# Diagonal of the keys' Gram matrix taken after the block gather; three shared buffers for split values and delta states; another bank for the first up unit

## The chip, the core and the metric

One core of a Trainium2 chip runs the whole kernel. The metric is device time in microseconds (us) of one execution; lower is better. Engines are named as in the profile: PE (TensorE; PEld its weight loads), DVE (VectorE), ACT (ScalarE), POOL (GpSimd) and SP (SyncE, which issues nearly all DMAs here).

## What is computed

A trunk of two layers (DEPTH = 2) on 512 tokens of width 1024, in float32. Each layer projects the normalised input into the parts of two branches: a gated delta rule (8 heads of 128, chunks with a triangular solve) and windowed attention (16 query heads, 2 key heads of 64, window 128). Both are projected up, gated, merged and projected out; an MLP with squared ReLU follows.

```python
def hybrid_layer(x, positions, ...):
    h = rmsnorm(x, pre_mix_g)
    proj = h @ w_in
    y_a = deltanet_branch(dn_q, dn_k, dn_v, dn_z, dn_b, dn_a, ...) @ w_up_dn
    y_b = swa_sink_branch(sw_q, sw_k, sw_v, positions, sw_sinks) @ w_up_sw
    mix = (jax.nn.sigmoid(gate_a) * y_a + jax.nn.sigmoid(gate_b) * y_b) @ w_o
    x = x + rmsnorm(mix, post_mix_g)
    h2 = rmsnorm(x, pre_mlp_g)
    ff = jnp.square(jax.nn.relu(h2 @ w_ff1)) @ w_ff2
    return x + rmsnorm(ff, post_mlp_g)

def deltanet_branch(...):
    k = l2norm(k.reshape(B, S, DN_HEADS, DN_DK))
    beta = jax.nn.sigmoid(b_in.astype(jnp.float32))

def gated_delta_rule(q, k, v, g, beta):
    kb = k * beta[..., None]
    L = jnp.where(strict, jnp.einsum('bhnid,bhnjd->bhnij', kb, k) * decay, 0.0)
    u = lax.linalg.triangular_solve(L, v * beta[..., None], ...)
```

The length of each key enters through l2norm: the keys' squares are the diagonal of the key Gram matrix K K^T, and `cj` is beta divided by (square + EPS).

## The kernel before

Weights stream from HBM through five buffers `wr`; ACT casts each to `wh` (L323), DVE makes the rest `wl = wr - wh` (L324), and PE multiplies three times per 128 rows of contraction (L339 to L341), up to four weight pieces ahead (`LOOK`). A unit of 24 matmuls of 128x512 yields a 128x512 block in a PSUM bank. Banks come from four pools: `PM` (2), `PS` (3), `PZ` (2), `PK` (1). The framework's scheduler sets the order of instructions on each engine from data dependences; within an engine they then run in that order, so a waiting instruction holds what is behind it. The SP queue likewise.

In each layer the part that the change touches runs so:

- **Block loop** (16 attention groups: 4 token tiles, 2 key heads, 2 halves). Beside each group run units from the list `MIX`: K (keys of one head, `k_unit`, L722 on), G and GA (gates). `k_unit(h)` projects and convolves the keys, reloads the decay matrix `D`, makes the Gram blocks on PE (`ps_a`, L735, the only bank of `PK`), then on DVE takes the four diagonals with a multiplication by the identity (L740), adds EPS (L742), takes `irk` by a power on POOL (L744), makes `cj` (L747, L748), scales the four blocks by `cj` and `D` into `uu` (L752) and sends `uu` to HBM (`ud`).
- An attention group makes scores on PE (`ps_s`, L892), masks them into `M` (DVE L896 or ACT L899 with DVE L900), takes maximum, exponential, sum and reciprocal (DVE L904 to L913, ACT L910), scales `M` on ACT (L916), transposes it on PE (`ps_pt`, L922), splits it (`pf`, L411, L412) and multiplies by the split values `vp` (`ps_o`, L938). `att_prep(t)` (L838) makes `vp` for the tile, in two buffers.
- **Solve** (L780 on): all 32x32 diagonal blocks are gathered as `ub` (L783) and inverted by 31 DVE steps, spread over the last attention groups, the first dense units and the eight up units of attention (`ps_us`, L1211 on).
- **Chain** (8 heads): `d_load` brings the blocks of `ud` back as `ur`, `d_inverse` completes the inverse on PE (`ps_i`) with POOL copies (L1048 to L1052), `d_chain` runs the recurrence with states `St` (four buffers of 128x128) and uses `cj` and `irk` as scales, while `d_dense` runs the value, query and gate projections of the next head.

The second layer repeats all this.

Of the kernel before, what the change touches and what calls it, by code (L numbers as in the profile page):

```python
# [20 lines left out]
P = 128  # L21
# [4 lines left out]
H = 8  # L26
# [93 lines left out]
def hybrid_trunk(ctx, tc, x, positions, pre_mix_g, dn_conv_w, dn_a_log, dn_dt_bias, dn_norm_g,  # L120
# [138 lines left out]
    vxd = dr.tile([H, P, 512], F32, name="vxd")  # L259
    gd = dr.tile([32, P], F32, name="gd")  # L260
    sd = dr.tile([H, 512], F32, name="sd")
    fd = dr.tile([H, 512], F32, name="fd")
# [257 lines left out]
    for l in range(depth):  # L520
# [130 lines left out]
        hc = lambda a: a.rearrange("p (h c) -> p h c", c=NC)  # L651
        beta = s1("beta", 32)
        act(out=hc(beta), in_=ba[:, :, 0:8].rearrange("p t h -> p h t"), func=AF.Exp, scale=-1.0)
# [18 lines left out]
        tt(out=hc(lw), in0=hc(lw), in1=nal.unsqueeze(2).broadcast_to([P, H, NC]), op=ALU.mult)  # L672
        gc, ngc, neg, egl = (s1(n_, 32) for n_ in ("gc", "ngc", "neg", "egl"))

        def decays():
            ps = PS("ps_g")
            mm(ps[:, 0:32], lhsT=le, rhs=lw, start=True, stop=True)
            nc.vector.tensor_copy(gc, ps[:, 0:32])
            ts(out=ngc, in0=gc, scalar1=-1.0, scalar2=None, op0=ALU.mult)
            act(out=neg, in_=gc, func=AF.Exp)  # L680
            ts(out=neg, in0=neg, scalar1=-1.0, scalar2=None, op0=ALU.mult)
            ps = PS("ps_gt")
            tr(ps[:32, :P], gc, ident)
            gT = sm.tile([32, P], F32, name="gT", bufs=1)
            nc.vector.tensor_copy(gT, ps[:32, :P])
            dma(gd, gT)
            egT = sm.tile([32, P], F32, name="egT", bufs=1)
            act(out=egT, in_=gT, func=AF.Exp)
            dma(egd, egT)
            for h in range(H):  # L690
                d = T[4 + h % 2]("D")
                dma(c4(d), gd[h * NC:(h + 1) * NC, :].partition_broadcast(P))
                nc.gpsimd.affine_select(out=c4(d), in_=c4(d), pattern=[[0, NC], [1, P]],
                                        compare_op=ALU.is_ge, fill=NEG, base=0, channel_multiplier=-1)
                act(out=egl[:, h * NC:(h + 1) * NC], in_=c4(d)[:, :, P - 1], func=AF.Exp)
                for c in range(NC):
                    act(out=d[:, c * P:(c + 1) * P], in_=d[:, c * P:(c + 1) * P], func=AF.Exp,
                        bias=ngc[:, h * NC + c:h * NC + c + 1])
                dma(dd[h], d)
# [21 lines left out]

        cj, irk = [], []  # L722

        def k_unit(h):
            ps = PM("ps_kp")
            mm_a(ps, hT)
            k_ = conv_silu(ps, 8 + h, T[4], "kk")
            dma(kkd[h], k_)
            yield
            d = T[5]("D")  # L730
            dma(d, dd[h])
            ps = PK("ps_a")
            for c in range(NC):
                sl = slice(c * P, (c + 1) * P)
                mm(ps[:, sl], lhsT=k_[:, sl], rhs=k_[:, sl], start=True, stop=True)  # L735
            u_ = T[5]("uu")
            sk_ = sm.tile([P, NC], F32, name="ssk")
            for c in range(NC):
                sl = slice(c * P, (c + 1) * P)
                stt(out=u_[:, sl], in0=ps[:, sl], scalar=1.0, in1=ident, op0=ALU.mult,  # L740
                    op1=ALU.mult, accum_out=sk_[:, c:c + 1])
            ts(out=sk_, in0=sk_, scalar1=EPS, scalar2=None, op0=ALU.add)  # L742
            ir = sm.tile([P, NC], F32, name="irk", bufs=H + 1)
            ptt(out=ir, in0=sk_, in1=phalf, op=ALU.pow)  # L744
            irk.append(ir)
            cc = sm.tile([P, NC], F32, name="cj", bufs=H + 1)
            nc.vector.reciprocal(cc, sk_)  # L747
            tt(out=cc, in0=cc, in1=hc(beta)[:, h, :], op=ALU.mult)  # L748
            cj.append(cc)
            for c in range(NC):  # L750
                sl = slice(c * P, (c + 1) * P)
                stt(out=u_[:, sl], in0=ps[:, sl], scalar=cc[:, c:c + 1], in1=d[:, sl],  # L752
                    op0=ALU.mult, op1=ALU.mult)
            dma(umat(h), c4(u_))
# [25 lines left out]
        def solve():  # L780
            ub = X4("ub")
            u0 = ud[:, :]
            dma(ub.rearrange("p (j i) -> p j i", j=32),  # L783
                bass.AP(u0.tensor, u0.offset, [[32 * P + 32, P], [P, 32], [1, 32]]))
            pb = X4("pb")
            nc.gpsimd.memset(pb, 0.0)
            nc.gpsimd.memset(pb[:, 0:1024:33], 1.0)
            yield
            uv = ub.rearrange("p (j i) -> p j i", j=32)
            pv = pb.rearrange("p (n i) -> p n i", n=32)  # L790
            for j in range(30, -1, -1):
                m = 31 - j

                for n0, n1 in (((0, m),) if m <= 16 else ((0, (m + 1) // 2), ((m + 1) // 2, m))):
# [7 lines left out]
                                            op=ALU.add, negate=True)  # L802
                yield
            dma(pd, pb)
            Pc, Tc = X4("Pc"), X4("Tc")
# [26 lines left out]

        def att_prep(t):
            tsl = slice(t * P, (t + 1) * P)
            kd = kv[t]

            vp = sm.tile([P, 512], F32R, name="vp")
            v4 = lambda a: a.rearrange("p (g r d) -> p r g d", g=2, r=2)  # L838
# [3 lines left out]
            for a, src in ((vp[:, 0:256], v_), (vp[:, 256:512], kd[:, 256:384]))[:1 + (t > 0)]:  # L842
                a, src = v4(a), src.rearrange("p (g d) -> p g d", g=2)
                split(src, a[:, 0], a[:, 1])
            at["v", t] = vp
            ps = PS("ps_k")
            tr(ps[:, 0:P], kd[:, 0:128], ident)
# [142 lines left out]
        def d_load(*hs):  # L990
            for h in hs:
                if h < H:
                    dma(uview(h), umat(h))

        def d_inverse(h):
# [84 lines left out]
        def d_turn(h):  # L1080
            d, k_ = dn["D", h], dn["k", h]
            kds = sm.tile([P, NC], F32, name="kds")
            tc.keep_in_program_order(tt(out=kds, in0=cj[h], in1=c4(d)[:, :, P - 1], op=ALU.mult))
            dn["k", h] = k_, by_token(k_, kvx[1][:, h % 2 * 512:(h % 2 + 1) * 512], kxd[h]), kds
# [59 lines left out]
        def d_chain(h):  # L1144
# [8 lines left out]
            for c in range(NC):  # L1153
                sl = slice(c * P, (c + 1) * P)
                stt(out=aT[:, sl], in0=ps[:, sl], scalar=cj[h][:, c:c + 1], in1=d[:, sl],
                    op0=ALU.mult, op1=ALU.mult)
# [3 lines left out]
            for c in range(NC):  # L1160
                for out_, in_, by in ((vs, vt, irk[h]), (kd, kt, kds)):
                    act(out=out_[:, c * P:(c + 1) * P].rearrange("p (a i) -> p a i", a=4),
                        in_=in_[:, :, c, :], func=AF.Copy, scale=by[:, c:c + 1])
            order.end()
            po = PZ("ps_o")
            St = None
            for c in range(NC):
# [14 lines left out]
                if c < NC - 1:  # L1182
                    pu = PS("ps_su")
                    mm(pu[:, 0:P], lhsT=kd[:, sl], rhs=yy, start=True, stop=True)
                    S2 = sm.tile([P, P], F32, name="St", bufs=4)
                    if c == 0:
# [23 lines left out]
        for m in range(KT):  # L1210
            ps = PM("ps_us")  # L1211
            mm_a(ps, oT)
# [253 lines left out]
```

## Time and profile before

| | |
|---|---|
| three runs, median (lowest to highest) | 1831.02 us (1830.64 to 1831.49) |
| the profiled execution's own time | 1830.59 us |
| its span, first to last instruction | 1828.6 us |
| granted TensorE clock | 0.999 |
| busy: PE, DVE, ACT, POOL | 99%, 71%, 51%, 12% of the span |
| block loop and solve in layer 0 | about 78 to 300 us of the span |

The span is what the trace covers; the execution's own time has 1.99 us around it. Matmuls overlap in PE's pipeline, so a PE that reads as busy can still start its matmuls later than it could. What PE loses is read from the distance between starts: in an undisturbed run of 128x512 matmuls it is 0.23 us.

### The profile page before, as it was taken

What the parts mean: (1) busy time and instruction counts of PE and PEld (TensorE: products, weight loads), DVE (VectorE), ACT (ScalarE), POOL (GpSimd) and SP (SyncE); (2) the same over time, 40 slices, a digit from 0 to 9 for tenths busy, and PEclk for the clock granted to TensorE, in tenths of its full rate; (3) what the DMA queues carried; (4) which work ended last, traced back from release to release, by engine and by line L of the source; (5) the groups of instructions that cost most, each with busy time, mean ns of one, the idle gap of its engine ahead of it and who ended that gap; (6) DMA issues with size and microseconds to landing.
All of it is one profiled execution on the core that took longest, in us unless ns stands there. A gap on an engine that the chain in (4) does not pass through costs nothing.

```text
span 1828.6 us, 26748 instructions
## 1 busy us (share of the span) xinstructions
PE 1809.1 (99%) x9598; PEld 1503.9 (82%) x9598; DVE 1292.1 (71%) x2466; ACT 940.9 (51%) x1913; POOL 211.2 (12%) x386
## 2 busy tenths in 40 slices
PE   9999999999999999999999999999999999999998
PEld 8888778888788888888898887888887898888886
DVE  5499796887566758684556997968885568585934
ACT  6678742444434645544347877234444346554442
POOL 0322102221101000000003221022111010000000
PEclk9999999999999999999999999999999999999999
DMA  5633447554453363564245343485545534544631
GB/s 188 202 118 116 115 149 223 179 170 149 124 191 124 96 216 120 168 217 151 93 151 181 104 127 110 167 234 165 160 139 153 172 119 135 174 163 148 233 102 46
DMA packets 146422, 278.48 MB, mean 152 GB/s; under 512 B 33569, under 2 KB 66657, under 8 KB 146290
## 3 DMA queue, kind: packets, MB, share of 16 engines
q1 hardware_dynamic: 145778, 276.75, 47.4%
q8 instruction: 75, 1.23, 0.3%
q14 instruction: 57, 0.47, 0.1%
q0 software_dynamic: 512, 0.03, 0.0%
HBM read 239.38 MB, written 37.36 MB: 151 GB/s over the span
## 4 chain that ended last, share of the span: by engine, by line
PE 84%; DVE 6%; ACT 5%; DMA 3%; issue 1%; POOL 1%; SPq 0%; POOLq 0%; DVEq 0%; ACTq 0%
PE ps_f L340 6%; PE ps_f L339 6%; PE ps_f L341 6%; PE ps_p L402 3%; PE ps_p L404 3%; PE ps_p L400 3%; PE ps_b L388 3%; PE ps_b L387 3%; PE ps_b L389 3%; PE ps_vp L339 2%; PE ps_us L339 2%; PE ps_ud L339 2%; PE ps_vp L341 2%; PE ps_ud L341 2%; PE ps_ud L340 2%; PE ps_us L340 2%
## 5 line engine op out<-in xcount | busy, mean ns | idle before, releaser
L323 ACT CAST wh<-wr 128x1024 fp32r<-128x1024 f32 (+1 forms) x332 | 343.1, 1040 | 542.2 <-PE ps_f L340 145.8
L324 DVE TENSOR_TENSOR wl<-wr,wh 128x1024 fp32r<-128x1024 f32 (+1 forms) x332 | 400.4, 1216 | 303.6 <-ACT wh L323 300.6
L339 PE MATMUL ps_f<-g_h,wh 128*128 128x512 f32 x448 | 174.3, 389 | 0.0
L340 PE MATMUL ps_f<-g_l,wh 128*128 128x512 f32 x448 | 174.3, 389 | 0.0
L341 PE MATMUL ps_f<-g_h,wl 128*128 128x512 f32 x448 | 174.3, 389 | 0.0
L402 PE MATMUL ps_p<-wl,P_h 128*128 128x512 f32 x336 | 131.4, 391 | 0.4 <-DVE wl L324 0.3
L404 PE MATMUL ps_p<-wh,P_l 128*128 128x512 f32 x336 | 130.8, 389 | 0.0
L400 PE MATMUL ps_p<-wh,P_h 128*128 128x512 f32 x336 | 129.5, 389 | 0.0
L437 POOL TENSOR_TENSOR pr<-pq,pw 128x1 f32<-128x1 f32 x16 | 9.8, 613 | 807.6 <-DVE pq L436 807.6
L339 PEld LDWEIGHTS ps_f<-g_h,wh 128*128 128x128 f32 x448 | 84.1, 188 | 17.4
L341 PEld LDWEIGHTS ps_f<-g_h,wl 128*128 128x128 f32 x448 | 84.1, 188 | 17.4
L340 PEld LDWEIGHTS ps_f<-g_l,wh 128*128 128x128 f32 x448 | 84.1, 188 | 17.4
L402 PEld LDWEIGHTS ps_p<-wl,P_h 128*128 128x128 f32 x336 | 63.1, 188 | 15.8 <-DVE wl L324 2.4
L400 PEld LDWEIGHTS ps_p<-wh,P_h 128*128 128x128 f32 x336 | 63.1, 188 | 13.3
L404 PEld LDWEIGHTS ps_p<-wh,P_l 128*128 128x128 f32 x336 | 63.1, 188 | 12.8
L387 PE MATMUL ps_b<-wh,h_h 128*128 128x432 f32 (+1 forms) x192 | 71.1, 370 | 0.0
L388 PE MATMUL ps_b<-wl,h_h 128*128 128x432 f32 (+1 forms) x192 | 70.5, 367 | 0.3 <-DVE wl L324 0.3
L389 PE MATMUL ps_b<-wh,h_l 128*128 128x432 f32 (+1 forms) x192 | 70.2, 366 | 0.0
L293 DVE TENSOR_TENSOR wr<-wr 128x1024 f32<-128x1024 f32 x48 | 58.0, 1220 | 2.6 <-DMA wr<-in_weights_dram 1.9
L340 PE MATMUL ps_qp<-h_l,wh 128*128 128x512 f32 x128 | 54.0, 422 | 0.0
L339 PE MATMUL ps_vp<-h_h,wh 128*128 128x512 f32 x128 | 53.9, 421 | 0.0
L341 PE MATMUL ps_vp<-h_h,wl 128*128 128x512 f32 x128 | 53.6, 419 | 0.0
(359 smaller groups left out, 4873.6 us busy)
## 6 DMA issues: line engine op xcount, KB each, us to landing
wr<-in_weights_dram SPq DMA_DIRECT2D x320, 512.0 KB, 3.5
wr<-in_weights_dram SPq DMA_DIRECT2D x24, 432.0 KB, 3.6
D<-dd SPq DMA_DIRECT2D x32, 256.0 KB, 3.2
xd<-xo SPq DMA_DIRECT2D x12, 512.0 KB, 2.8
xt<-xd SPq DMA_DIRECT2D x24, 256.0 KB, 3.7
D<-gd SPq DMA_DIRECT2D x16, 256.0 KB, 6.5
dd<-D SPq DMA_DIRECT2D x16, 256.0 KB, 3.9
kkd<-kk SPq DMA_DIRECT2D x16, 256.0 KB, 2.0
```

What stands on the lines that cost most here:

```text
L293: tt(out=held[j], in0=held[j], in1=part(i, k, j), op=ALU.add)
L323: nc.scalar.copy(wh[:, :w], wr[:, :w])
L324: sub(out=wl[:, :w], in0=wr[:, :w], in1=wh[:, :w].bitcast(F32), op=ALU.subtract)
L339: mm(ps, lhsT=wh[:, k, :], rhs=hi, start=k == 0, stop=False)
L340: mm(ps, lhsT=wh[:, k, :], rhs=lo, start=False, stop=False)
L341: mm(ps, lhsT=wl[:, k, :], rhs=hi, start=False, stop=k == KT - 1)
L387: mm(pss[t], lhsT=hi[:, tsl], rhs=wh[:, r, :], start=k == 0, stop=False)
L388: mm(pss[t], lhsT=hi[:, tsl], rhs=wl[:, r, :], start=False, stop=False)
L389: mm(pss[t], lhsT=lo[:, tsl], rhs=wh[:, r, :], start=False, stop=k == KT - 1)
L400: mm(pss[t], lhsT=hi[:, c], rhs=wh[:, r, :], start=first, stop=False, skip_group_check=onto)
L402: mm(pss[t], lhsT=hi[:, c], rhs=wl[:, r, :], start=False, stop=False, skip_group_check=onto)
L404: mm(pss[t], lhsT=lo[:, c], rhs=wh[:, r, :], start=False, stop=last, skip_group_check=onto)
```

## The change

- `k_unit` no longer takes the diagonals, `irk` and `cj`. DVE multiplies the four Gram blocks by `D` in one 128x512 operation, and the unscaled blocks go to HBM.
- `solve` adds EPS to the diagonal of the gathered blocks, makes the scale there (`sq`, 128x32) and scales `ub` by it in one 128x1024 operation. beta reaches that layout through HBM (`bd`, `bq`), the squares come back to the token layout through HBM (`nd`, then `gT`) and a PE transpose (`ps_nt`); `cj` and `irk` are then made for all heads at once, `irk` by one 128x32 power on POOL.
- `d_load` scales the four reloaded blocks of a head with four ACT operations.
- `vp` has three buffers and is made half a tile earlier (`att_values`); the delta states are slices of a tile in the same buffers.
- The first up unit's bank comes from `PS` rather than `PM`.

```diff
@@ decays
-            tr(ps[:32, :P], gc, ident)
+            tr(ps[:64, :P], gcb, ident)
...
+            dma(bd, gT[32:64])
@@ k_unit
-            sk_ = sm.tile([P, NC], F32, name="ssk")
-            for c in range(NC):
-                sl = slice(c * P, (c + 1) * P)
-                stt(out=u_[:, sl], in0=ps[:, sl], scalar=1.0, in1=ident, op0=ALU.mult,
-                    op1=ALU.mult, accum_out=sk_[:, c:c + 1])
-            ts(out=sk_, in0=sk_, scalar1=EPS, scalar2=None, op0=ALU.add)
-            ir = sm.tile([P, NC], F32, name="irk", bufs=H + 1)
-            ptt(out=ir, in0=sk_, in1=phalf, op=ALU.pow)
-            irk.append(ir)
-            cc = sm.tile([P, NC], F32, name="cj", bufs=H + 1)
-            nc.vector.reciprocal(cc, sk_)
-            tt(out=cc, in0=cc, in1=hc(beta)[:, h, :], op=ALU.mult)
-            cj.append(cc)
-            for c in range(NC):
-                sl = slice(c * P, (c + 1) * P)
-                stt(out=u_[:, sl], in0=ps[:, sl], scalar=cc[:, c:c + 1], in1=d[:, sl],
-                    op0=ALU.mult, op1=ALU.mult)
+            tt(out=u_, in0=ps, in1=d, op=ALU.mult)
             dma(umat(h), c4(u_))
@@ solve
+            bq = s1("bq", 32)
+            dma(bq, bd.rearrange("g (b j) -> (g b) j", b=4))
...
+            sq = s1("ssq", 32)
+            ts(out=sq, in0=ub[:, 0:1024:33], scalar1=EPS, scalar2=None, op0=ALU.add)
+            dma(nd.rearrange("g (b j) -> (g b) j", b=4), sq)
+            nc.vector.reciprocal(sq, sq)
+            tt(out=sq, in0=sq, in1=bq, op=ALU.mult)
+            tt(out=uv, in0=uv, in1=sq.unsqueeze(2).broadcast_to([P, 32, 32]), op=ALU.mult)
+            nT = sm.tile([64, P], F32, name="gT", bufs=1)
+            dma(nT[0:32], nd)
...
+            ps = PS("ps_nt")
+            tr(ps[:, 0:32], nT[0:32], ident[:32, :32])
+            nc.vector.tensor_copy(irk, ps[:, 0:32])
+            nc.vector.reciprocal(cj, irk)
+            tt(out=cj, in0=cj, in1=beta, op=ALU.mult)
+            ptt(out=hc(irk), in0=hc(irk), in1=phalf.unsqueeze(1).broadcast_to([P, H, NC]), op=ALU.pow)
@@ attention
-            vp = sm.tile([P, 512], F32R, name="vp")
+            vp = sm.tile([P, 512], F32R, name="vp", bufs=3)
...
             if (g, e) == (1, 0) and t < NT - 1:
+                att_values(t + 1)
                 att_rope(t + 1)
@@ d_load
                     dma(uview(h), umat(h))
+                    for c in range(NC):
+                        act(out=uview(h)[:, c, :], in_=uview(h)[:, c, :], func=AF.Copy,
+                            scale=cj[:, h * NC + c:h * NC + c + 1])
@@ d_chain
+            states = sm.tile([P, 512], F32, name="St", tag="vp", bufs=3)
...
-                    S2 = sm.tile([P, P], F32, name="St", bufs=4)
+                    S2 = states[:, sl]
@@ up units
-            ps = PM("ps_us")
+            ps = (PM if m else PS)("ps_us")
```

The scheduler lays out the instructions anew. Three places, layer 0, with line numbers of each kernel.

**PE, around the transposes of the third attention group** (`ps_pt`; the units beside it make keys, `ps_kp`). The last score block ahead of them ends at row 436 in both programs. Before:

```order
448 L341 MATMUL ps_kp<-h_h,wl 128x512
449 L339 MATMUL ps_kp<-h_h,wh 128x512
450 L922 MATMUL ps_pt<-ident,M 128x128 x4
451 L340 MATMUL ps_kp<-h_l,wh 128x512
452 L341 MATMUL ps_kp<-h_h,wl 128x512
```

Now:

```order
443 L341 MATMUL ps_kp<-h_h,wh 128x512
444 L342 MATMUL ps_kp<-h_l,wh 128x512
445 L932 MATMUL ps_pt<-ident,M 128x128 x4
446 L343 MATMUL ps_kp<-h_h,wl 128x512
447 L341 MATMUL ps_kp<-h_h,wh 128x512
```

The four transposes stand five matmuls earlier behind the score block. Most of the later groups moved the same way.

**DVE, the first `k_unit` beside the third attention group** (`M` is that group's score tile, `uu` the scaled Gram block, `kk` the next head's keys). Before:

```order
99 L742 TENSOR_SCALAR ssk<-ssk 128x4
100 L866 SCALAR_TENSOR_TENSOR qT<-ps_q,qT 64x512
101 L714 SCALAR_TENSOR_TENSOR kk<-ps_kp,cw,kk 128x511
102 L747 RECIPROCAL cj<-ssk 128x4
103 L866 SCALAR_TENSOR_TENSOR qT<-ps_q,qT 64x512
104 L718 SCALAR_TENSOR_TENSOR kk<-th,kk 128x512
105 L748 TENSOR_TENSOR cj<-cj,beta 128x4
106 L896 TENSOR_TENSOR M<-ps_s,ban 128x256
107 L752 SCALAR_TENSOR_TENSOR uu<-ps_a,cj,D 128x128 x4
108 L896 TENSOR_TENSOR M<-ps_s,ban 128x256
```

Now:

```order
97 L741 TENSOR_TENSOR uu<-ps_a,D 128x512
98 L952 TENSOR_TENSOR qt_421<-ps_o,qt_421 64x512
99 L718 SCALAR_TENSOR_TENSOR kk<-ps_kp,cw,kk 128x509
100 L874 SCALAR_TENSOR_TENSOR qT<-ps_q,qT 64x512
101 L718 SCALAR_TENSOR_TENSOR kk<-ps_kp,cw,kk 128x510
102 L874 SCALAR_TENSOR_TENSOR qT<-ps_q,qT 64x512
103 L718 SCALAR_TENSOR_TENSOR kk<-ps_kp,cw,kk 128x511
104 L906 TENSOR_TENSOR M<-ps_s,ban 128x256 x2
105 L722 SCALAR_TENSOR_TENSOR kk<-th,kk 128x512
```

`uu`, which frees the Gram bank, moved from between the two score operations to ahead of the query splits, and the two score operations stand together.

**ACT, from the up units to the chain** (`wh` are weight casts, `ur` the reloaded blocks, `vs` the first chain's values). Before:

```order
287 L1111 ACTIVATE wq<-qq 128x512
288 L323 CAST wh<-wr 128x1024 x9
289 L772 ACTIVATE sga<-ps_ga 128x512
290 L323 CAST wh<-wr 128x1024
291 L772 ACTIVATE sga<-ps_ga 128x512
292 L1162 ACTIVATE vs<-kvx,irk 128x128
```

Now:

```order
281 L1124 ACTIVATE wq<-qq 128x512
282 L325 CAST wh<-wr 128x1024 x7
283 L1005 ACTIVATE ur<-ur,cj 128x128 x15
284 L325 CAST wh<-wr 128x1024
285 L760 ACTIVATE sga<-ps_ga 128x512
286 L1005 ACTIVATE ur<-ur,cj 128x128
```

The sixteen scalings of the first four heads stand around the cast that was the ninth after the queries' square. On SP, `nd<-ssq` and `gT<-nd` now stand behind `ub<-ud` and one weight load, ahead of one `gad` store and two weight loads; `bd<-gT` stands between `gd<-gT` and `egd<-egT`.

## Rows read from the trace of the kernel before

**Rows 1.** The page: busy time of each engine, share of the span, instructions.

```profile
PE 1809.1 (99%) x9598; PEld 1503.9 (82%) x9598; DVE 1292.1 (71%) x2466; ACT 940.9 (51%) x1913; POOL 211.2 (12%) x386
```

**Rows 2.** Waits of PE, whole span: us in total, times, longest us.

```profile
PE ps_pt L922 <- ACT M L916: 3.9, 6, 0.8
...
PE ps_us L339 <- DVE qq L714: 0.6, 2, 0.3
...
PE ps_a L735 <- DVE uu L752: 0.5, 2, 0.2
...
PE ps_s L892 <- DVE M L900: 0.4, 1, 0.4
...
PE ps_b L388 <- DVE wl L324: 0.3, 1, 0.3
```

**Rows 3.** Stretches of layer 0: us, busy PE, PEld, DVE, ACT, POOL; clock; DMA.

```profile
78.00:110.00 32.00, 30.21 (x161) 24.51 (x160) 28.14 (x81) 22.21 (x70) 6.84 (x13) 1.00 0.34 103
110.00:150.00 40.00, 39.93 (x215) 32.94 (x214) 37.40 (x103) 34.81 (x101) 8.15 (x12) 1.00 0.36 118
```

**Rows 4.** Timeline of PE: start us, us, engine, line; in brackets idle before and releaser.

```profile
100.69 0.22 PE L892 MATMUL ps_s<-kT_h,qT 128*128 128x128 f32 x1
101.13 1.16 PE L735 MATMUL ps_a<-kk 128*128 128x128 f32 x8 [0.22 <-DVE uu L752]
...
107.06 0.66 PE L922 MATMUL ps_pt<-ident,M 128*128 128x128 f32 x4 [0.75 <-ACT M L916]
...
202.05 0.66 PE L922 MATMUL ps_pt<-ident,M 128*128 128x128 f32 x4 [0.51 <-ACT M L916]
...
245.57 0.39 PE L341 MATMUL ps_zp<-h_h,wl 128*128 128x512 f32 x1
246.25 0.47 PE L339 MATMUL ps_us<-oT_h,wh 128*128 128x512 f32 x1 [0.28 <-DVE qq L714]
246.55 0.40 PE L340 MATMUL ps_us<-oT_l,wh 128*128 128x512 f32 x1
246.79 0.39 PE L341 MATMUL ps_us<-oT_h,wl 128*128 128x512 f32 x1
```

**Rows 5.** Groups by line and shape, whole span: busy us, mean ns, idle before.

```profile
L740 DVE SCALAR_TENSOR_TENSOR uu<-ps_a,ident 128x128 f32<-128x128 f32 x64 | 16.1, 282 | 1.7 <-PE ps_a L735 0.8 <-issue 0.8
L752 DVE SCALAR_TENSOR_TENSOR uu<-ps_a,cj,D 128x128 f32<-128x128 f32 x64 | 17.8, 340 | 0.1
L412 DVE TENSOR_TENSOR pf_l<-ps_pt,pf_h 128x512 fp32r<-128x512 f32 x32 | 21.8, 682 | 1.8 <-ACT pf_h L411 1.5
L324 DVE TENSOR_TENSOR wl<-wr,wh 128x1024 fp32r<-128x1024 f32 x308 | 375.5, 1229 | 259.0 <-ACT wh L323 256.2 <-PE ps_pt L922 2.3
L1162 ACT ACTIVATE vs<-kvx,irk 128x128 f32<-128x128 f32 x64 | 25.0, 390 | 3.5 <-DMA kvx<-vxd 3.5
L744 POOL TENSOR_TENSOR irk<-ssk,pw 128x4 f32<-128x4 f32 x16 | 18.1, 1129 | 109.7 <-DVE ssk L742 107.3 <-DVE den L913 2.3
L437 POOL TENSOR_TENSOR nr<-nq,pw 128x1 f32<-128x1 f32 x16 | 10.6, 662 | 45.3 <-DVE nq L436 45.3
```

**Rows 6.** Timelines of SP and ACT where the blocks are gathered (start us, us).

```profile
193.13 0.36 SPq L783 DMA_DIRECT2D ub<-ud  x1
196.44 3.42 SPq L274 DMA_DIRECT2D wr<-in_weights_dram  x2
...
208.62 1.03 ACT L323 CAST wh<-wr 128x1024 fp32r<-128x1024 f32 x1
```

**Rows 7.** The chain that ended last: start us, us, a small DMA of layer 1.

```profile
1298.54 2.22 DMA ff<-sd
```

**Rows 8.** Timelines of SP, ACT, POOL and PE where the chain begins (start us, us).

```profile
287.12 2.07 SPq L993 DMA_DIRECT2D ur<-ud  x4
...
295.28 1.06 ACT L323 CAST wh<-wr 128x1024 fp32r<-128x1024 f32 x1 [4.38 <-PE ps_ga L340]
...
294.15 2.59 POOL L1050 COPY Pt<-Pc 32x128 f32<-32x128 f32 x8
...
300.84 0.21 PE L1018 MATMUL ps_i<-Tc,ur 32*32 32x32 f32 x1
```

More of the change, by code (lines that the diff above doesn't have):

```diff
@@ L260, in hybrid_trunk @@
     gd = dr.tile([32, P], F32, name="gd")
+    bd = dr.tile([32, P], F32, name="bd")
+    nd = dr.tile([32, P], F32, name="nd")
     sd = dr.tile([H, 512], F32, name="sd")
@@ L651, in hybrid_trunk @@
         hc = lambda a: a.rearrange("p (h c) -> p h c", c=NC)
-        beta = s1("beta", 32)
+        gcb = s1("gcb", 64)
+        gc, beta = gcb[:, 0:32], gcb[:, 32:64]
         act(out=hc(beta), in_=ba[:, :, 0:8].rearrange("p t h -> p h t"), func=AF.Exp, scale=-1.0)
@@ L672, in hybrid_trunk @@
         tt(out=hc(lw), in0=hc(lw), in1=nal.unsqueeze(2).broadcast_to([P, H, NC]), op=ALU.mult)
-        gc, ngc, neg, egl = (s1(n_, 32) for n_ in ("gc", "ngc", "neg", "egl"))
+        ngc, neg, egl = (s1(n_, 32) for n_ in ("ngc", "neg", "egl"))
         def decays():
@@ L682, in decays @@
             ps = PS("ps_gt")
-            tr(ps[:32, :P], gc, ident)
-            gT = sm.tile([32, P], F32, name="gT", bufs=1)
-            nc.vector.tensor_copy(gT, ps[:32, :P])
-            dma(gd, gT)
+            tr(ps[:64, :P], gcb, ident)
+            gT = sm.tile([64, P], F32, name="gT", bufs=1)
+            nc.vector.tensor_copy(gT, ps[:64, :P])
+            dma(gd, gT[0:32])
+            dma(bd, gT[32:64])
             egT = sm.tile([32, P], F32, name="egT", bufs=1)
-            act(out=egT, in_=gT, func=AF.Exp)
+            act(out=egT, in_=gT[0:32], func=AF.Exp)
             dma(egd, egT)
@@ L719, in conv_silu @@
             return a
-        cj, irk = [], []
+        irk, cj = s1("irk", 32), s1("cj", 32)
         def k_unit(h):
@@ L831, in att_rope, with att_values @@
                 ptt(out=x2, in0=tm[2], in1=tm[3], op=ALU.add)
-        def att_prep(t):
-            tsl = slice(t * P, (t + 1) * P)
+        def att_values(t):
             kd = kv[t]
-            vp = sm.tile([P, 512], F32R, name="vp")
+            vp = sm.tile([P, 512], F32R, name="vp", bufs=3)
             v4 = lambda a: a.rearrange("p (g r d) -> p r g d", g=2, r=2)
@@ L845, in att_prep @@
             at["v", t] = vp
+        def att_prep(t):
+            tsl = slice(t * P, (t + 1) * P)
+            kd = kv[t]
             ps = PS("ps_k")
@@ L874, in att_group @@
                     att_rope(0)
+                    att_values(0)
                 att_prep(t)
             if (g, e) == (1, 0) and t < NT - 1:
+                att_values(t + 1)
                 att_rope(t + 1)
@@ L1082, in d_turn @@
             kds = sm.tile([P, NC], F32, name="kds")
-            tc.keep_in_program_order(tt(out=kds, in0=cj[h], in1=c4(d)[:, :, P - 1], op=ALU.mult))
+            tc.keep_in_program_order(tt(out=kds, in0=hc(cj)[:, h, :], in1=c4(d)[:, :, P - 1], op=ALU.mult))
             dn["k", h] = k_, by_token(k_, kvx[1][:, h % 2 * 512:(h % 2 + 1) * 512], kxd[h]), kds
@@ L1154, in d_chain @@
                 sl = slice(c * P, (c + 1) * P)
-                stt(out=aT[:, sl], in0=ps[:, sl], scalar=cj[h][:, c:c + 1], in1=d[:, sl],
+                stt(out=aT[:, sl], in0=ps[:, sl], scalar=cj[:, h * NC + c:h * NC + c + 1], in1=d[:, sl],
                     op0=ALU.mult, op1=ALU.mult)
@@ L1160, in d_chain @@
             for c in range(NC):
-                for out_, in_, by in ((vs, vt, irk[h]), (kd, kt, kds)):
+                for out_, in_, by in ((vs, vt, irk[:, h * NC:(h + 1) * NC]), (kd, kt, kds)):
                     act(out=out_[:, c * P:(c + 1) * P].rearrange("p (a i) -> p a i", a=4),
```

## Prediction

> **What bounds the kernel now.** I read the page's busy times first: PE is busy for 99% of the span, DVE for 71%, ACT for 51% [rows 1]: PE is the bound. So the end moves only by what PE no longer waits for, or has to do more. Next I read what PE waits for [rows 2]: of the waits that the change can touch, the transposes `ps_pt` behind ACT's scaled scores are 3.9 us in six times, three in each layer, and the others are some tenths: the first up unit 0.6, the Gram blocks 0.5, a score block 0.4, a projection matmul 0.3. Idle time by the profile is a little too small, since it is counted from modelled ends; the distance between starts tells the rest, and there an undisturbed 128x512 matmul takes 0.23 us (246.55 to 246.79 is 0.24) [rows 4]. Last I read who is full where PE waits. In the block loop that is DVE: 28.14 of 32 us and 37.40 of 40 us, 88 and 94%, while ACT has 31 and 13% free [rows 3]. The reader is to see two things: DVE is nearly full in the block loop, so that its order decides when scores are ready; and yet PE loses very little to it, about 6 us in both layers. That is all there is to win, and it is 0.3% of the time.
>
> **The change, part by part.**
>
> *Less on DVE in `k_unit`.* Out go 64 products with the identity, 282 ns each, and 64 scaled products, 340 ns each: 16.1 + 17.8 = 33.9 us in both layers. In come 16 products of 128x512 out of PSUM; the nearest row is the split of the transposed scores, 682 ns, so 10.9 us [rows 5]. DVE is relieved of 23.0 us, 1.4 us for each of 16 units, besides three operations on 128x4 in each, and POOL of 18.1 us of powers. Most of that was never on PE's path. What was:
> - The Gram blocks wait for their single bank, which DVE's scaled products empty: the score matmul starts at 100.69 and the Gram block at 101.13 [rows 4]. `uu` now comes far ahead of that, in one operation. PE's idle time there is 0.22; with the modelled end I count 0.3 a layer, **-0.6**.
> - The third group's transposes start 0.75 us late at 107.06 [rows 4]. Between this group's two score operations and its reciprocal stood one unit's scaled products and the next unit's diagonals: 4 x 0.340 + 4 x 0.282 = 2.5 us, of which one 0.68 us operation is left, so 1.8 us less. But the scheduler has moved the transposes five matmuls, 1.15 us, nearer to the scores. 1.8 - 1.15 leaves 0.65 us; bounds are 0 (the relief lies beside the chain) and 0.75. I take 0.6, near the upper end, because the products stand on the very chain, **-1.2** for two layers.
> - The wait of a score block for DVE's masks, 0.4 us, once, in layer 1 [rows 2]: **-0.4**.
> - The transposes at 202.05, 0.51 us late [rows 4], stand beside the start of the solve; see there.
>
> *The first up unit's bank.* Its first matmul starts 0.68 us after the last of the gate projection, against 0.23, waiting for the query convolution to leave the bank (the releaser is `qq`) [rows 4]. In another pool it does not wait: 0.45 x 2 = **-0.9**. Next in line is the second up unit, which needs the same release, but 5.5 us later.
>
> *Diagonal and scale in the solve.* Added on DVE: three operations on 128x32 and one on 128x1024, for which the weight split of the same size stands, 1229 ns [rows 5]. They come where DVE has just lost the last unit's 1.8 us. Per layer the transposes at 202.05 can gain their 0.51 or lose up to 1.23 us; I take 0, as relief and addition are about equal. The solve itself ends as early or late as before within 1 us, with idle DVE behind it.
>
> *The way through HBM on the SP queue.* The store of the squares waits for the gather's landing and DVE, the load waits for the store, and one `gad` store and two weight loads stand behind both. The gather is issued at 193.13, the weight loads at 196.44 to 199.86, and the cast that begins the next weights runs at 208.62 [rows 6]. A small DMA of the chain takes 2.22 us [rows 7]. Store and load hold SP for about that each, so the second weight load comes perhaps 2 us later and lands still before 208.62. The Trainium skill, page "DMA: Bandwidth & Descriptors", section "Anatomy of one DMA — SWDGE (gpsimd) path", speaks against this edit: a DMA has a fixed cost of about 2.0 us, mostly the wait for the receipt, and a semaphore wait is served on the issuing sequencer, so what stands behind it waits too. By that rule the hold would be, as an estimate from that page, 4.0 us; the sum would be the same, and this case's 2.22 us agrees with the size. By the rows alone: two times 2.22 us, cover about 5 us, cost **0**; without that cover 1 to 2 us a layer.
>
> The other new store, of beta, stands ahead of the decay matrices' loads: one issue on SP, about 0.36 us as for `ub` [rows 6]. In layer 1 a projection matmul waits 0.3 us for a weight split that stands behind the decay work on ACT and DVE [rows 2], and it gets later by that: **+0.3** (0 to 0.4).
>
> *`irk` for all heads on POOL.* A power takes 662 ns on 128x1 and 1129 on 128x4 [rows 5], 156 ns a column, so 128x32 would take 0.66 + 31 x 0.156 = 5.5 us, or in proportion to 128x4 8 x 1.13 = 9.0 us. It stands ahead of POOL's copies for the inverse, which ended at 294.15 + 2.59 = 296.74; PE's first `ps_i` is at 300.84 [rows 8]. That one reads the solve's tile and the reloaded blocks, not POOL's copies, which serve the inverse steps behind it. 5.5 us later the copies end at 302.2, 9.0 us later at 305.7: **0**, and about 1 us a layer if the later steps need them sooner than I think.
>
> *Scaling on ACT.* 32 operations a layer of 128x128, like `vs` at 390 ns [rows 5], 12.5 us; ACT is about half busy. The sixteen of the first four heads, 6.2 us, have to lie between the landing of `ur` (issued at 287.12 to 289.19, landed some 2.2 us later) and 300.84, which is 9 us, together with one cast of 1.06 us. That cast had been waiting 4.38 us for PE to free its buffer [rows 8], and its weights are used some units later, so its delay of about 2 us is covered: **0**. Without that room, 1 us. The later heads' scalings have a whole head's time.
>
> *Buffers.* Three for `vp`, made earlier, and the states as slices of a tile: no PE operation is added, and no wait for these stands in the rows: **0**.
>
> *More breaks on PE.* PE's program has 22 more rows of the order, two of them the new transposes: its long runs are broken oftener. After a change of kind the next matmul takes 0.30 instead of 0.23 to 0.24 us (246.25, 246.55, 246.79) [rows 4], so at most 22 x 0.07 = 1.5 us, at least 0; I take **+0.6**.
>
> **The sum**: -0.6 - 1.2 - 0.4 - 0.9 + 0.3 + 0.6 = -2.2 us. The profiled execution took 1830.59 us (its span of 1828.6 and 1.99 around it), the median of the runs is 0.43 above it. 1830.59 - 2.2 = 1828.4, and by the median **1828.8 us**, or 0.12% less.
>
> **Rivals.**
> *A: DVE's relief reaches all of PE's waits.* For it: DVE at 88 to 94%, and 23 us taken off it. Against: one of the three late `ps_pt` of a layer comes ahead of the first Gram block, and the programme order is tightened as well. Then the second and third `ps_pt` go (2 x (0.75 + 0.51) = 2.5), the score, Gram and up-unit waits of rows 2 (1.5), some 0.15 us for each of these nine waits by start distance (1.3), and the breaks cost nothing, +0.3 for SP: -5.0, **1826.0 us**.
> *B: it does not show.* The scheduler spends all that DVE has gained by moving PE's transposes earlier, so PE waits as before. Left are the bank, -0.9, and SP and the breaks, +0.9: **1831.0 us**. For it: the transposes did move by 1.15 us, DVE's relief is 1.4 us a unit.
> *C: slower, by PE's program order.* PE runs strictly in its order, and in most groups the transposes now stand over 1 us nearer to their scores. Eight units relieve sixteen groups; where the relief falls beside the group's chain, PE stands at the transposes and all projections behind them wait too. The price of one is that of the row at 107.06, 0.75 us. Four groups in each layer make 8 x 0.75 = +6.0, with bank, SP and breaks 0 in sum: **1837.0 us**. It decides against the change when relief on the chain is under 1.15 us in more than about two groups a layer. Against it: PE waited in few groups until now, and the score-to-transpose distances had room.
>
> **How the numbers follow.** My forecast has 0.50, A 0.24, B 0.18, C 0.08. About 0.2% (3.7 us) is what a measurement of this kernel can tell from no change: faster is below 1827.4, slower above 1834.7. Faster: nine tenths of A and a fifth of the forecast's spread, 0.32. Slower: C and little else, 0.08. Same: 0.60. The range leaves out C and the outer half of A's spread: with the bounds (both `ps_pt` gone -1.3, breaks and SP -0.9; no gain at `ps_pt` +1.2, masks +0.4, dearer breaks +0.9) the forecast spans 1826.6 to 1831.3; A stretches it down to 1825.0, B and a part of the solve's bound up to 1832.0.
>
> **What would show it.** In the waits of PE the rows of `ps_a` and `ps_us` gone, `ps_pt` down from 3.9 to about 2.7, the one at 107.06 nearly gone and that of the first group unchanged; DVE busy in the block loop down by about 11 us a layer; the first `ps_i` not waiting for ACT; no weight split late behind SP at 210 us. Wrong it would be if `ps_pt` grew or appeared in new groups (C), if the chain's start waited for `ur`, POOL or SP, or if PE's sum of waits fell by over 4 us (A).

## The result, and the profile after

| | before | after |
|---|---|---|
| median of 7 runs, us | 1830.95 | 1836.89 |
| single runs, us | 1830.61 to 1831.49 | 1835.15 to 1838.95 |
| profiled execution, us | 1830.59 | 1838.95 |
| its span, us | 1828.6 | 1837.3 |

The ratio is 1.0033, with a 95% interval of 1.0023 to 1.0042: slower by 5.9 us, outside the range, and slower by more than the 0.2% that a measurement can tell. The single runs also spread over 3.8 us, those of before over 0.9; in the later rounds, though, 21 to 29 runs of before spread over 2.3 to 4.1.

The work went the way that was meant. First the page's busy times, to be read against [rows 1]: VectorE (DVE) lost 14.8 us, POOL 3.9, ACT gained 21.4, and PE, which sets the end, has as much to do as before.

```profile
PE 1810.5 (99%) x9600; PEld 1505.1 (82%) x9600; DVE 1277.3 (70%) x2256; ACT 962.3 (52%) x1977; POOL 207.3 (11%) x372
```

Next the waits of PE over the whole span, in us, times, and the longest, against [rows 2].

```profile
PE ps_o L948 <- POOL pc L942: 4.9, 4, 1.9
PE ps_o L948 <- DVE pf_l L414: 3.1, 5, 1.5
...
PE ps_pt L932 <- ACT M L926: 2.1, 4, 0.7
PE ps_y L1193 <- ACT vs L1175: 2.1, 2, 1.2
...
PE ps_y L1193 <- DVE rr L1190: 0.9, 1, 0.9
...
PE ps_b L390 <- DVE wl L326: 0.4, 1, 0.4
```

The waits that the change was to remove are gone or smaller: `ps_us`, `ps_a` and `ps_s` have no row any more, `ps_pt` fell from 3.9 to 2.1. Two rows that [rows 2] did not have stand above them: PE waits for POOL's masked probabilities `pc` and for DVE's low part `pf_l`, both at the value matmul `ps_o`. The two rows of `ps_y` were 1.1 and 0.4 us before; the longest of them now, 1.2 us, stands behind a load from HBM (`kvx<-vxd`), and no run takes it apart.

The timeline of PE (start us, us, engine, line; in brackets the idle time before and its releaser) shows the largest of them, once in each layer at the same place:

```profile
155.90 0.40 PE L948 MATMUL ps_o<-pc,vp 128*128 128x512 f32 x1
156.13 0.38 PE L739 MATMUL ps_a<-kk 128*128 128x128 f32 x2
158.38 0.50 PE L948 MATMUL ps_o<-pc,vp 128*128 128x512 f32 x1 [1.86 <-POOL pc L942]
158.71 0.38 PE L739 MATMUL ps_a<-kk 128*128 128x128 f32 x2
158.85 0.58 PE L341 MATMUL ps_kp<-h_h,wh 128*128 128x512 f32 x1
159.23 0.63 PE L342 MATMUL ps_kp<-h_l,wh 128*128 128x512 f32 x1
159.65 0.63 PE L343 MATMUL ps_kp<-h_h,wl 128*128 128x512 f32 x1
...
1067.70 0.50 PE L948 MATMUL ps_o<-pc,vp 128*128 128x512 f32 x1 [1.86 <-POOL pc L942]
1068.03 0.38 PE L739 MATMUL ps_a<-kk 128*128 128x128 f32 x2
1068.17 0.47 PE L341 MATMUL ps_kp<-h_h,wh 128*128 128x512 f32 x1
1068.48 0.39 PE L342 MATMUL ps_kp<-h_l,wh 128*128 128x512 f32 x1
1068.71 0.40 PE L343 MATMUL ps_kp<-h_h,wl 128*128 128x512 f32 x1
```

The chain that ended last, followed back through the first of these places (start us, us, what), says why: PE waits for one selection on POOL, and that stands behind ten operations of the rotation.

```profile
152.44 0.64 POOL pc L942
153.07 0.42 POOL rt L831
153.50 0.42 POOL rt L832
153.91 0.87 POOL rt L833
154.78 0.42 POOL rt L834
155.20 0.18 POOL rt L831
155.38 0.18 POOL rt L832
155.56 1.16 POOL rt L833
156.73 0.18 POOL rt L834
156.91 0.41 POOL qt L835
157.32 0.41 POOL qt L836
157.73 0.60 POOL pc L942
```

In the trace of before POOL's timeline at the same place (start us, us) has a power of `irk` (L744) in front of the rotation, and the second selection behind two operations of it only:

```profile
151.48 0.64 POOL L932 TENSOR_SCALAR_AFFINE_SELECT pc<-pf_h 128x512 fp32r<-128x512 f32 x1 [5.16 <-ACT pf_h L411]
152.22 1.01 POOL L744 TENSOR_TENSOR irk<-ssk,pw 128x4 f32<-128x4 f32 x1
153.19 0.46 POOL L826 TENSOR_TENSOR rt<-qt,cs 128x128 f32<-128x128 f32 x1
153.61 0.47 POOL L827 TENSOR_TENSOR rt<-qt,cs 128x128 f32<-128x128 f32 x1
154.35 0.64 POOL L932 TENSOR_SCALAR_AFFINE_SELECT pc<-pf_l 128x512 fp32r<-128x512 f32 x1 [0.27 <-DVE pf_l L412]
```

In the changed program that power is gone, and ten of the twelve operations of the last block's rotation stand ahead of the selection, which starts at 157.73 instead of 154.35. That the planner (the framework's scheduler) moved them up because the power went, and not because of what else the Gram part changes, is likely but not shown: no run takes out the power alone.

The idle time also has an echo. In stretches of layer 0 (busy us of PE, PEld, DVE, ACT, POOL; granted TensorE clock, 1.00 being full speed; DMA) the clock falls right behind it:

```profile
155.00:160.00 5.00, 3.14 (x16) 2.55 (x16) 3.58 (x6) 2.37 (x7) 3.69 (x10) 0.91 0.54 188
160.00:165.00 5.00, 5.00 (x22) 4.34 (x21) 4.03 (x15) 3.00 (x14) 0.00 (x0) 0.75 0.24 74
```

That is the lower level, 1.2 GHz, for a part of both stretches: in the timeline above two matmuls start 0.42 us apart (159.23, 159.65), and in layer 1 0.23 (1068.48, 1068.71). What is missing to full speed is 5 x 0.09 + 5 x 0.25 = 1.7 us. Behind the same idle time in layer 1 the clock did not fall, and there the fourteen matmuls that follow took 2.42 us (1068.17 to 1070.59) where layer 0 took 3.96 (158.85 to 162.81): 1.5 us more at the lower clock. From start to start PE loses about 2.03 us in each layer (156.13 to 158.38 is 2.25 us, for two Gram blocks that take about 0.2). So these two places and the clock make 5.6 to 5.8 us of the 8.4 by which the profiled execution, the dearest of the seven, lies above that of before; the rest was not taken apart.

A last place is in layer 1, at the solve. DVE's timeline:

```profile
1105.74 0.19 DVE L782 TENSOR_SCALAR ssq<-ub 128x32 f32<-128x32 f32 x1
...
1110.90 0.35 DVE L784 RECIPROCAL ssq<-ssq 128x32 f32<-128x32 f32 x1 [3.67 <-DMA nd<-ssq]
...
1114.91 0.68 DVE L414 TENSOR_TENSOR pf_l<-ps_pt,pf_h 128x512 fp32r<-128x512 f32 x1
```

The reciprocal overwrites `sq`, which the store `nd<-ssq` still reads, so DVE waits until the store has landed, 4.84 us after its issue at 1106.06 (3.27 us in layer 0). `pf_l` is queued behind, and PE's longest wait for `pf_l`, 1.5 us, is there.

So there were three suspects: POOL's queue (theory P), with the clock behind it; DVE's wait for the store (theory W); and, nearest to the rival of the prediction, PE's changed order as a whole (theory O). Theory S, the stretching of POOL's operations, came out of the first experiment.

### The profile page after: what moved, and what is told of

Read it like the earlier page. It is cut to its first block, busy times and chain, and to the rows that moved or that the text cites. A ratio compares the mean times of both kernels' runs of the same rounds, so it can differ in the third digit from the quotient of the medians.

```text
span 1837.3 us, 26599 instructions
## 1 busy us (share of the span) xinstructions
PE 1810.5 (99%) x9600; PEld 1505.1 (82%) x9600; DVE 1277.3 (70%) x2256; ACT 962.3 (52%) x1977; POOL 207.3 (11%) x372
## 4 chain that ended last, share of the span: by engine, by line
PE 86%; DVE 5%; ACT 3%; DMA 3%; POOL 1%; issue 1%; SPq 0%; POOLq 0%; DVEq 0%; ACTq 0%
PE ps_f L341 6%; PE ps_f L342 6%; PE ps_f L343 6%; PE ps_p L404 4%; PE ps_p L406 4%; PE ps_p L402 4%; PE ps_b L390 3%; PE ps_b L389 3%; PE ps_b L391 3%; PE ps_vp L341 2%; PE ps_us L341 2%; PE ps_ud L341 2%; PE ps_us L342 2%; PE ps_ud L342 2%; PE ps_ud L343 2%; PE ps_us L343 2%
```

## The experiments

Each run is compared with runs of the kernel before on the same chip; "x1.0015 [1.0006, 1.0024]" is the ratio to it with its 95% interval. The rounds ran on different chips, with medians of before from 1830.2 to 1831.2 us, so kernels of different rounds are compared by their ratios.

**1. The rotation behind the selection.** The changed kernel with an order, no semaphore, on POOL:

```diff
         def att_rope(t):
+            def ptt(**k):
+                nc.gpsimd.tensor_tensor(**k)
+                if t == 3:
+                    tc.add_manual_dep(nc.cur_bb.bb.instructions[-1], at["pc"].name, ...)
...
+                    if (t, g, e) == (1, 1, 1):
+                        at["pc"] = nc.cur_bb.bb.instructions[-1]
                     pvs.append((at["v", t], 256, b))
```

> The changed kernel with POOL's order put back in one place of each layer: the last block's rotation (L831 to L836) starts only behind the mask selection pc<-pf_l of the last group of the second block. Theory P (the loss is POOL's queue): the two idle times of PE of 2.03 us at ps_o<-pc go, with them the 3.4 us at half granted clock in layer 0, some 1.7 us: 1836.9 - 3.6 - 1.7 = 1831.6 us, within 1830.8 to 1832.6, and the spread of the single runs shrinks from 3.8 us to about 1. Theory W (the loss is VectorE's wait for the store of the squares): nothing of it is touched, PE loses at the next place what it gains here, 1835.5 us or more. Theory O (the loss lies in PE's changed program order as a whole): the same, 1835.5 or more.

Measured: 1833.75 us, x1.0015 [1.0006, 1.0024]. The clock stays at 1.00 in both stretches, and about half of the loss is gone, by one order on an engine that is busy for 11% of the span. So neither theory W nor theory O, which wanted 1835.5 us or more, is the whole of the loss. Theory P missed too: it wanted 1831.6 us, and it wanted a spread of the single runs of about 1 us, which stayed at 4.4 (1831.68 to 1836.11). The wait did not vanish, it halved. PE's, POOL's and DVE's timelines of this run:

```profile
156.87 0.50 PE L955 MATMUL ps_o<-pc,vp 128*128 128x512 f32 x1 [0.90 <-POOL pc L947]
```

```profile
155.25 1.56 POOL L947 TENSOR_SCALAR_AFFINE_SELECT pc<-pf_l 128x512 fp32r<-128x512 f32 x1 [2.47 <-DVE pf_l L414]
```

```profile
154.49 0.69 DVE L414 TENSOR_TENSOR pf_l<-ps_pt,pf_h 128x512 fp32r<-128x512 f32 x1
155.10 1.22 DVE L326 TENSOR_TENSOR wl<-wr,wh 128x1024 fp32r<-128x1024 f32 x1
156.35 0.69 DVE L879 SCALAR_TENSOR_TENSOR qT<-ps_q,qT 64x512 fp32r<-64x512 f32 x1
```

The selection takes 1.56 us instead of 0.64. Beside it DVE runs a weight split, whose two operands both lie in SBUF; in the kernel before, `pf_l` and products out of PSUM stood there. This gave theory S. In the changed kernel the same split stands beside the rotation step of 1.16 us (155.56 in the chain above), and that step ends at 156.72, right behind the split's 156.64:

```profile
155.42 1.22 DVE L326 TENSOR_TENSOR wl<-wr,wh 128x1024 fp32r<-128x1024 f32 x1
```

The traces of all fourteen kernels hold 672 of these selections. The 374 with no DVE operation on two SBUF operands beside them took 0.62 to 0.66 us, and each of the 100 that took longer than 0.68 (up to 1.84) had one beside it. Not every such neighbour costs: the other 198 had one for a part of their time and took 0.62 to 0.67.

**2 and 3. A tile of its own for the reciprocal**, in the changed kernel and on top of experiment 1:

```diff
-            nc.vector.reciprocal(sq, sq)
-            tt(out=sq, in0=sq, in1=bq, op=ALU.mult)
+            rs = s1("ssr", 32)
+            nc.vector.reciprocal(rs, sq)
+            tt(out=rs, in0=rs, in1=bq, op=ALU.mult)
```

(and `rs` for `sq` in the scaling of `uv`.)

> The changed kernel with a tile of its own for the reciprocal of the squares, so that VectorE does not wait for the store that still reads them. Theory W: VectorE's waits of 2.10 and 3.67 us at L784 go and with them PE's 1.63 us at ps_o<-pf_l in layer 1: 1836.9 - 1.6 = 1835.3 us (1834.5 to 1836.0). Theory P: that store costs PE nothing else, most of the loss stays: 1835 to 1837 us with the 2 us at ps_o<-pc in both layers. A rival to both: without the wait the solve's scaling and its first small steps stand ahead of the masks' copies, and a ps_pt of 0.7 to 1.2 us appears in each layer: 1837 to 1839 us.

> Both edits together, the later rotation and the tile of its own. If theories P and W name two separate losses: 1836.9 - 5.3 - 1.6 = 1830.0 us (1829.0 to 1831.2), at or just under the kernel before. If W is nothing: 1831.6. If O is right: 1834 or more.

Measured: 1837.09 us, x1.0035 [1.0022, 1.0049], and 1833.93 us, x1.0017 [1.0008, 1.0025]: no gain over 1.0033 and 1.0015, though the first interval is wider than the 1.6 us (0.0009) in question. DVE does not wait for the store any more, and yet theory W's gain does not show. Part of why stands in PE's waits of experiment 2, where a new row has come beside the smaller one for `pf_l`, as the solve's steps now stand ahead of the group's mask copies:

```profile
PE ps_o L949 <- DVE pf_l L414: 1.6, 4, 0.6
...
PE ps_o L949 <- ACT pf_h L413: 0.6, 2, 0.4
```

The rest stands in experiment 1, which still has the store and the reciprocal in one tile. There DVE waits for the store, 4.3 us in both layers, and PE has no wait for `pf_l` at the solve, its longest being 0.6:

```profile
DVE ssq L784 <- DMA nd<-ssq: 4.3, 2, 2.2
...
PE ps_o L955 <- DVE pf_l L414: 1.7, 4, 0.6
```

So experiment 3 had nothing to win there over experiment 1. The 3.67 us wait and PE's 1.5 us behind it are shown for one execution of the changed kernel; how often they come is open.

**4. The first up unit's bank alone**, in the kernel before:

```diff
-            ps = PM("ps_us")
+            ps = (PM if m else PS)("ps_us")
```

> The kernel before with nothing but the first up unit's accumulator in the other pool. The forecast's term: 0.45 us in each layer gone, 1831.0 - 0.9 = 1830.1 us. The rival: the wait passes to the second up unit or to another user of that pool, 1831.0 us.

Measured: 1829.78 us, x0.9993 [0.9984, 1.0002]: 1.4 us less, with an interval from 2.9 less to 0.4 more. That holds both the forecast's 0.9 and the rival's nothing, so the run does not tell them apart. No kernel of this study was measurably faster than the one before. Its profile shows `ps_us` without a wait, and in that execution nearly all of it given back a little earlier: the selection ahead of it took 1.17 us instead of 0.76 beside DVE's `oT_l` splits, and PE's two value matmuls there start 0.96 us apart instead of 0.55, which is 0.41 of the 0.45 us. The order there is the same in both kernels, and experiment 6, without the bank, has the same 0.57 us wait in one layer, so the bank is not what makes it.

**5, 6 and 8. One part alone**, in the kernel before: the Gram diagonals (the diff without `vp`, `states` and the bank), the early values (only those), and the values with the bank. The values' part is:

```diff
-        def att_prep(t):
+        def att_values(t):
...
-            vp = sm.tile([P, 512], F32R, name="vp")
+            vp = sm.tile([P, 512], F32R, name="vp", bufs=3)
...
+                att_values(t + 1)
                 att_rope(t + 1)
...
+            states = sm.tile([P, 512], F32, name="St", tag="vp", bufs=3)
...
-                    S2 = sm.tile([P, P], F32, name="St", bufs=4)
+                    S2 = states[:, sl]
```

> The kernel before with the Gram diagonal's part alone: products on VectorE, squares through HBM, scaling in the solve, powers and scalings in one piece; the split values stay in their place with two buffers, the states in their own tiles, the first up unit in its old pool. Theory P (POOL's queue): by POOL's order the rotation already stands ahead of the selection in this part alone, so the 2 us at ps_o<-pc and the half clock behind it are there in full: 1835 to 1838 us. Rival V (it is the values made early that fill VectorE and POOL at the wrong place): 1829 to 1832 us.

> The kernel before with the split values a block early in three buffers shared with the states, and nothing else. POOL's order is that of before. Theory P: no idle time of 2 us, 1830 to 1832 us, no change to speak of. Rival V: 1834 us or more.

> The kernel before with the two parts that do not touch the Gram blocks: values early and the first up unit's bank. If the Gram part carries the loss: 1829 to 1831 us, at or under the kernel before, with the bank's 0.45 us a layer half given back at the selection at the end of the block loop. If values early cost: over 1832 us.

Measured: Gram alone 1835.56 us, x1.0026 [1.0015, 1.0037], with both long waits and the half clock; values alone 1833.09 us, x1.0015 [1.0007, 1.0024]; values and bank 1831.69 us, x1.0006 [0.9997, 1.0015]. So the Gram part carries most of the loss, as theory P has it. Theory P was wrong of the values: alone they cost too. That the cost is the wait below is likely but not shown, since the values with the bank have the same row and no cost clear of noise. PE's waits with the values alone show

```profile
PE ps_gb L339 <- DVE kk L714: 2.3, 2, 1.1
```

once in each layer: a projection waits for its bank, which DVE's key convolution empties later.

**7. The split later**, on top of experiment 1 (`hold` is filled in `att_q` of the first group of the third block, and meets the second weight split written after that):

```diff
             sub(out=wl[:, :w], in0=wr[:, :w], in1=wh[:, :w].bitcast(F32), op=ALU.subtract)
+            if hold:
+                hold[1] -= 1
+                if not hold[1]:
+                    tc.add_manual_dep(nc.cur_bb.bb.instructions[-1], hold[0].name, ...)
+                    hold.clear()
...
+            if (t, g) == (2, 0):
+                hold.extend([nc.cur_bb.bb.instructions[-1], 2])
```

> The kernel of the first experiment (rotation behind the selection) with one order more: the weight split wl that VectorE runs straight behind pf_l of the same group comes behind the split of the transposed queries. Theory S (the selection on POOL is stretched from 0.64 to 1.56 us because VectorE's split out of SBUF runs beside it): the selection takes 0.65 to 0.9 us, PE's remaining 1.06 us at ps_o<-pc falls to 0.2 to 0.4 in both layers, 1833.8 - 1.5 = 1832.3 us (1831.3 to 1833.2). If the selection is just slow there: 1.5 us as before and 1833.0 to 1834.5. Since the planner places other work differently behind the later split, the time can also move by about 1 us by that; the duration of the selection decides.

Measured: 1831.14 us, x1.0003 [0.9994, 1.0011]: 0.9 us above before, no difference that can be measured. The selection and PE behind it:

```profile
155.43 0.64 POOL L956 TENSOR_SCALAR_AFFINE_SELECT pc<-pf_l 128x512 fp32r<-128x512 f32 x1 [2.46 <-DVE pf_l L421]
```

```profile
155.42 0.50 PE L964 MATMUL ps_o<-pf_l,vp 128*128 128x512 f32 x1
155.76 0.86 PE L964 MATMUL ps_o<-pc,vp 128*128 128x512 f32 x2
```

The selection takes 0.64 us and PE has no idle time by the profile: theory S holds. In time it is 1.0015 - 1.0003 = 0.12%, 2.2 us; the two intervals overlap a little, but the rows say the same, for from start to start experiment 1 lost 1.06 us at this place in each layer. The split now runs at 159.98 instead of 155.10.

**10. The split later alone**, without the order on POOL (the diff of experiment 7 in the changed kernel).

> The changed kernel with the later split alone; the rotation stays ahead of the selection on POOL. Tells POOL's order from the stretching: with no split beside them the ten rotation operations take about 3.7 us instead of 5.2 and the selection starts some 1.4 us earlier. Theory P plus S: PE's idle time at ps_o<-pc falls from 2.03 to 0.5 to 0.9 us in both layers, the granted clock does not drop, 1832 to 1833.3 us, dearer than the seventh experiment by 0.5 to 1.5. If the order alone counts: 2 us and the half clock stay, 1835 to 1837 us. If the stretching alone counts: as the seventh, 1831 us.

Measured: 1833.62 us, x1.0016 [1.0007, 1.0025]. The ten operations took 153.09 to 156.81, 3.7 us instead of 4.7 (not 5.2, as the expectation has it), and PE's idle time is

```profile
157.50 0.50 PE L957 MATMUL ps_o<-pc,vp 128*128 128x512 f32 x1 [0.94 <-POOL pc L951]
```

with the clock at 1.00. Each order alone takes back about half (x1.0015 and x1.0016), both together all but 0.03%: two causes in series, not one. The rows add up to that: each order alone takes about 1 us off PE's loss of 2.03 in each layer, and the 1.5 to 1.7 us of the lower clock with it, together some 3.5 us against 3.3 and 3.1 by the ratios.

**9. Without the early values**: experiment 7's kernel with `vp` back in `att_prep`, two buffers, and the states in their own tiles.

> The kernel of the seventh experiment (rotation behind the selection, split later) with the values put back in their old place and two buffers, so Gram part, bank and the two orders. If the early values cost as much here as alone (1.5 to 2.9 us): 1831.1 - 2 = 1829 us, under the kernel before. If in the changed kernel they cost nothing, since VectorE has been relieved: 1831 us as in the seventh.

Measured: 1831.79 us, x1.0007 [0.9998, 1.0016], as the seventh within the intervals: in the changed kernel the early values cost nothing that can be measured.

**11 and 12. A group's second half first**, on experiments 7 and 9, for the wait at `ps_o<-pf_l`, which is 0.56 us by the profile at 101.62 in the changed kernel:

```diff
             g = att_group(*groups[i])
+            if i == 2:
+                fin(late)
             next(g)
             fin(late)
```

> The seventh experiment's kernel (both orders mended) with one more: in the third turn of the block loop the second half of the group before (transposes, pf, values) is written ahead of the next group's scores, so that VectorE makes pf_l before the score masks and not 4 us after its transposes. Theory O' (what is left of the loss is PE standing at ps_o<-pf_l at 101 us, 0.73 us a layer, because its transposes come earlier but VectorE's split behind them does not): that wait goes, 1831.1 - 1.4 = 1829.7 us (1829.0 to 1830.5), under the kernel before by a half to one. If the wait only moves to ps_pt or the next group: 1831 us or more.

> The same edit on the ninth experiment's kernel (both orders mended, values in their old place). Theory O': 1831.8 - 1.4 = 1830.4 us. If values early cost nothing and O' is right, as the eleventh within 0.7; if O' is wrong, 1831.8 us.

Measured: 1831.79 us, x1.0006 [0.9997, 1.0015], and 1831.67 us, x1.0008 [0.9999, 1.0017]. No gain. PE's waits in the eleventh:

```profile
PE ps_pt L946 <- ACT M L940: 5.5, 6, 1.7
...
PE ps_o L964 <- DVE pf_l L421: 0.5, 2, 0.3
```

The wait at `pf_l` fell from 1.6 us in four times (experiment 7) to 0.5, and the one at the next group's transposes grew from 2.7 to 5.5: the scores that were put behind came too late. Theory O' named a real wait, but not one that this order can win.

## Why the prediction was wrong

**The step that failed** stands in the first paragraph of "Less on DVE in `k_unit`": DVE is relieved "and POOL of 18.1 us of powers. Most of that was never on PE's path." The price of a removed operation was taken as at most nothing lost. I did not read POOL's order in the block loop, since POOL was busy for 12% of the span. But with the Gram part (experiment 5 has it alone) ten rotation operations slid ahead of a selection for which PE waits, about 2.03 us a layer from start to start; with the rotation put back behind it, 1.06 us are left (experiment 1). The power stood in front of the rotation, and its going is the likely reason for the new order. The prediction looked at POOL's queue where a power is added, ahead of the inverse, and not where sixteen are taken away.

**The second failure** is in the same sentence, for DVE. What it loses is work out of PSUM, and what now stands there is a weight split out of SBUF, which stretches POOL's operations beside it (experiments 7 and 10). No term of the sum had a price that depends on what runs on another engine. Together with the clock (1.5 to 1.7 us in the profiled run) the two made 3.3 us (1.0033 to 1.0015 for POOL's order) and 2.2 us (to 1.0003 for the split).

The terms one by one:

- *PE is the bound, only its waits count*: right.
- *Gram bank, -0.6*: the wait is gone [rows 4], but PE's program puts the value matmul in front of the Gram blocks, and that waits 0.56 us for `pf_l` at 101.62. Given back in full.
- *Third group's transposes, -1.2*: idle 0.32 us at 106.08 instead of 0.75 [rows 4]. About 0.4 a layer instead of 0.6. The first group's 0.73 stayed, as foretold.
- *Diagonal and scale in the solve, 0*: the late transposes at 202.05 [rows 4] have no row any more in either layer, about 0.5 us each won; in layer 1 the 1.5 us wait for `pf_l` came in that place.
- *Score wait, -0.4, and the up unit, -0.9*: both rows are gone, but a selection just ahead of the up unit makes PE wait 0.56 us in each layer. The bank alone measured -1.4 (-2.9 to +0.4 by the interval).
- *The store of beta, +0.3*: `ps_b` waits 0.4 us instead of 0.3 [rows 2]; less than taken.
- *The way through HBM, 0*: I looked at who stands behind the store on SP and not at who waits for it on DVE. The store alone took 3.27 and 4.84 us until it landed, against 2.22 [rows 7] in the sum. The rule of the Trainium skill that was set against this edit, of about 2.0 us a DMA ("DMA: Bandwidth & Descriptors", section "Anatomy of one DMA — SWDGE (gpsimd) path"), is too small here as well; the page gives it for DMAs that GpSimd issues, and these go out from SP. Experiments 2 and 3 found no gain without DVE's wait for the store, so nothing speaks against the 0 by time, though in the profiled execution PE lost 1.5 us behind it.
- *`irk` on POOL and scaling on ACT, 0*: right. The power took 5.4 us a layer and the 64 scalings 392 ns each, and PE has no row that waits for either.
- *Buffers, 0*: wrong for the values alone (experiment 6), right within the changed kernel (experiment 9).
- *Breaks on PE, +0.6*: not measured apart.

**The rivals.** C had the sign and even the sum, 1837.0, but not the mechanism: `ps_pt`, where it put the loss, fell from 3.9 to 2.1 us, so its number came out right by luck. A had the waits of [rows 2] going: `ps_us`, `ps_a` and `ps_s` did and `ps_pt` by half, but it missed what came in their place. I had given 0.08 to slower, all of it for waits that I could already see in the old profile.

## What to carry to other kernels

Before an operation is called free to remove, look at what the planner moves into its place, on that engine and above all on nearly idle ones: an engine at 12% with one result that PE waits for is on the path. Compare the order of every queue, the emptier first, and look for a consumer of PE's behind the work that moved up. And price an operation on GpSimd by what VectorE does beside it: here a 0.64 us selection took up to 1.84, and moving one split behind it, from 155.10 to 159.98, was worth about 2 us.

## What the runs showed of the hardware

- **DVE and POOL hold each other up.** A rotation step of 128x16 took 1.16 us instead of 0.18 and a selection 1.56 instead of 0.64 beside DVE's split of 1.22 us, whose operands both lie in SBUF; beside `pf_l` or `qT`, which read PSUM, POOL kept its 0.64. The Trainium skill, page "SBUF — State Buffer", section "SBUF: two separate sides", says that the two engines share a pair of ports and that whichever starts first, a VectorE operation with two SBUF inputs or one of GpSimd, holds it for the whole instruction. The traces agree: in experiment 1 the split started at 155.10 and ended at 156.32, and the selection issued at 155.25 ended at 156.81, 0.49 us behind it. It goes the other way as well: in the changed kernel a selection that started at 186.13 kept its 0.64 us, and the split issued at 186.25 took 1.59 us instead of 1.22.
- **An idle time of 2 us on PE can cost nearly as much again.** In the three profiles with the 2 us wait left in layer 0 (the changed kernel, experiments 2 and 5) the granted clock went to 1.2 GHz behind it, each time in layer 0 and never in layer 1, where the same wait stands. With the wait at 1.1 us or less (experiments 1, 3, 7 and 10) it stayed at 2.4 GHz. The lists of all executions agree: the mean granted clock was 0.998 or less in 14 of the 19 executions of the three kernels with the 2 us wait, and in 1 of the 110 of the other ten experiments. What tells the two layers apart, or the executions, was not found.
